# One order of query blocks for another: alternating block sizes, a longer look-ahead and later output units in an attention and mixture-of-experts kernel

## The chip, the cores and the metric

The kernel runs on one NeuronCore of one Trainium2 chip. The metric is the device time of one execution in microseconds. Every time below is from runs of the kernel before the change, or from one execution of it that the profiler recorded.

## What is computed

One layer: forgetting attention (softmax attention with a bias c[t]-c[s], the running sum of log-sigmoid forget gates), an output gate, a normalisation, a mixture of experts with top-2 routing, and a second normalisation. S = D = 1024, 16 heads of 64. The part that the change touches:

```python
proj = h @ w_in
q, k, v, f_logit, o_logit = jnp.split(...)
log_f = jax.nn.log_sigmoid((f_logit + b_f).astype(jnp.float32))
c = jnp.cumsum(log_f, axis=1)
...
logits = einsum('bqhd,bkhd->bhqk', q_i, k) * scale + c_i[..., :, None] - c[:, :, None, :]
logits = jnp.where(key_pos[None, :] <= q_pos[:, None], logits, -jnp.inf)
p = jax.nn.softmax(logits, axis=-1)
return einsum('bhqk,bkhd->bqhd', p, v)
...
o = merge_blocks(o) * jax.nn.sigmoid(o_logit)
return o @ w_out
```

## The kernel before

The values of all heads are computed first (`front`). Then `pairs` goes through eight pairs of heads (`hp` 0 to 7), and in each through eight query blocks of 128 rows (`i`) for each of the two heads (`j`): 16 steps a pair, 128 in all. A block `i` sees `i+1` blocks of 128 keys, so a block 7 has eight times the work of a block 0. Below, (hp: i,j) names a block, as (2: 0,0).

A block goes through two functions. `attn_s` (line 362) forms the logits with TensorE in a PSUM tile `sp` (two of these are there), takes their minimum on VectorE (`mn`; the sign of the logits is turned), takes the exponential on ScalarE (`s`), makes a high and a low fp16 part (`hl`: the copy of line 378 on ScalarE, the subtraction of line 379 on VectorE) and issues a DMA transpose of it from SyncE into `pT` (line 381). `attn_o` (line 385) multiplies `pT` with the values. Four blocks (two `i`, two `j`) share a PSUM tile `ops`; after the fourth, the group is finished: reciprocal `ro` and product `ox` on VectorE (lines 403 and 405), the gate on GpSimd (line 407), a copy `gh` on ScalarE (line 409), a subtraction `gl` on GpSimd (line 410). `ox` has one buffer. Two steps later, two DMA transposes (line 414, called "the turn" here) write the group into `oTh` and `oTl`, which the output projection reads.

The order is one list, `todo`. Blocks are started `LA` = 4 steps ahead of their `attn_o`, in `start`. Between the two, `fill` puts in TensorE units of 0.66 us each, by a running budget: in pairs 0 to 6 the projections of the next pair (`proj_units`: queries, keys, gates; two PSUM tiles `pj`), whose results `evac` (line 336) takes to SBUF with ScalarE and VectorE; in the last pair the first output units (`out_units`), half a row of tiles 0 to 3 each. An output unit with k = 7 needs `oTh` and `oTl` of the last pair, and carries its tile's number; `fill` takes it once `turned[7]` holds that number, that is once the turn has been issued. `later` holds work for a later step: the turns, the loads of weights two pairs ahead (`load_w`), and their splits (`load_split`).

```python
todo = [(hp, i, j) for hp in range(NP) for i in ((0,1,6,7,2,3,4,5) if hp < NP - 1 else range(NT)) for j in range(2)]
...
for n, (hp, i, j) in enumerate(todo):
    start(n + LA)
    ...
    due -= self.fill(due)
    self.now = n
    ...
    self.attn_o(hp, i, j, ready.pop(n), ps)
```

The framework keeps the order of each engine's own instructions fixed when the kernel is built; each engine works its list off in that order and waits at an instruction until what it needs is there. SyncE issues nearly all DMAs, the transposes among them, in one such list. `bias_rows` (line 288) fills four bias tiles once, before the first pair. `mid_begin` (line 477), before the last pair, loads and splits what follows attention. After attention come the rest of the output projection, the routing and the experts, whose weights are streamed in from HBM by DMAs that stand behind the last turn on SyncE.

Of the kernel before, what the change touches and what calls it, by code (L numbers as in the profile page):

```python
# [28 lines left out]
PS = 16384.0  # L29
VW = 2 * HD + 2  # L30
CW = (16.0, 2.0 ** -4, 2.0 ** -12)
BIG = 1e30
# [4 lines left out]
QG = 2  # L37
# [21 lines left out]
class Kern:  # L59
# [18 lines left out]
    def fill(self, us):  # L78
        done = 0
        while us > done and self.fill_q:  # L80

            at = next((n for n, u in enumerate(self.fill_q) if len(u) < 3 or u[2] in self.turned[NP - 1]), None)
            if at is None:
                break
            c, f = self.fill_q.pop(at)[:2]
            f()
            done += c
        return done
# [165 lines left out]
    def load_w(self, hp, step=None):  # L254
        nc = self.nc
        at = 0
        for n, off in self.QKG:
            h = self.wp.tile([128, KT, 128], F16, name="wh", bufs=3)
            l = self.wp.tile([128, KT, 128], F16, name="wl", bufs=3)
            self.W[hp, n] = (h, l)  # L260
            for c in range(2):
                def load(n=n, off=off, c=c):
                    r = self.wp.tile([128, 4, 128], F32, name="wr", bufs=3)
                    ks = slice(4 * c, 4 * c + 4)
                    nc.sync.dma_start(r, self.w_k[:, ks, off + hp * 128:off + (hp + 1) * 128])
                    return self.W[hp, n][0][:, ks, :], self.W[hp, n][1][:, ks, :], r
                if step is None:
                    self.split(*load(), WS, "pool")
                else:
                    self.load_split(load, step + (0, 2, 6, 8, 11, 13)[at])  # L270
                at += 1


    def load_split(self, load, step):
        def late(tiles):
            with self.tc.issue_after(self.mn.ins), self.tc.issue_after(self.gated.ins):
                self.split(*tiles, WS, "pool")
        self.later.append((step - 4, lambda: self.later.append((step, lambda t=load(): late(t)))))
# [9 lines left out]
    def bias_rows(self):  # L288
        nc, wk = self.nc, self.wk
        w = wk.tile([3, 2, S], F16, name="cw", tag="s", bufs=3)  # L290
        for n, sign in enumerate((1.0, -1.0)):
# [6 lines left out]
        for q, k in zip(self.QB, self.KX):  # L298
            for j in range(2):
                o = (1 - j) * 64  # L300
                nc.gpsimd.memset(q[o:o + 64, j, :], 0.0)
                nc.vector.memset(k[o:o + 64, 2 * j + 1, :], 0.0)
                nc.sync.dma_start(q[o:o + 3, j, :], w[:, 0, :])
                nc.sync.dma_start(k[o + 3:o + 6, 2 * j + 1, :], w[:, 1, :])
# [57 lines left out]
    def attn_s(self, hp, i, j, ps):  # L362
# [11 lines left out]
        self.mn = nc.vector.tensor_reduce(mn, sp[:, :n], axis=AX, op=OP.min)  # L374
        s = wk.tile([128, S], F32, name="s", bufs=3)
        nc.scalar.activation(s[:, :n], sp[:, :n], AF.Exp, scale=-1.0, bias=mn)  # L376
        hl = wk.tile([128, 2 * S], F16, name="hl", bufs=3)[:, :2 * n]
        nc.scalar.activation(hl[:, :n], s[:, :n], AF.Copy, scale=PS)  # L378
        nc.vector.scalar_tensor_tensor(hl[:, n:], s[:, :n], PS, hl[:, :n], op0=OP.mult, op1=OP.subtract)  # L379
        pT = wk.tile([128, 2 * NT, 128], F16, name="pT", bufs=5)[:, :2 * (i + 1), :]  # L380
        nc.sync.dma_start_transpose(pT, hl)
# [3 lines left out]
    def attn_o(self, hp, i, j, pT, ps):  # L385
# [3 lines left out]
        if i % nb == 0 and j == 0:  # L389
            self.o_ps = ps.tile([128, QG, 2, HD + 1], F32, name="ops", bufs=2)  # L390
        V = self.V[hd // 8]
        vo = hd % 8 * VW
        vh, vl = slice(vo, vo + HD + 1), slice(vo + HD + 2, vo + VW)
        o = self.o_ps[:, i % nb, j, :]
        for b in range(i + 1):
# [3 lines left out]
        if j == 0 or i % nb < nb - 1:  # L399
            return  # L400
        T = self.o_ps[:, :nb]
        r = wk.tile([128, QG, 2, 1], F32, name="ro", bufs=2)[:, :nb]
# [9 lines left out]
        def turn():  # L412
            for g, oT in ((gh, self.oTh), (gl, self.oTl)):
                nc.sync.dma_start_transpose(oT[:, hp, ts].rearrange("p (a b) -> p a b", b=128),
                                            g.rearrange("p a b c -> p (a b c)"))
            self.turned[hp].add(i)
        self.later.append((self.now + 2, turn))

    def pairs(self, ps):
        LA = 4  # L420
        self.bias_rows()
        self.later = []
        todo = [(hp, i, j) for hp in range(NP) for i in ((0,1,6,7,2,3,4,5) if hp < NP - 1 else range(NT)) for j in range(2)]
        per = len(todo) // NP
# [9 lines left out]
        def start(n):  # L434
            if n < len(todo):
                hp = todo[n][0]
                if n % per == 0:
                    while len(self.fill_q) > gates:
                        self.fill(0.1)
                    if hp + 1 < NP:  # L440
                        self.load_c(hp + 1)
                        if hp + 2 < NP:
                            self.load_w(hp + 2, n - LA + 11)
                        self.fill_q += self.proj_units(hp + 1)
# [27 lines left out]
        while self.later:  # L472
            self.later.pop(0)[1]()
        self.flush()

# [794 lines left out]
    def run(self):  # L1270
        tc, nc, I = self.tc, self.nc, self.I
        self.w_k = I["fox_w_in"].rearrange("a d c -> (a d) c").rearrange("(k p) c -> p k c", p=128)
        self.W, self.QA, self.SG = {}, {}, {}
        self.turned = [set() for _ in range(NP)]
        self.wo, self.OP = [None, None], {}
# [109 lines left out]
```

## Time and profile before

| | |
|---|---|
| runs shown | 1170.14, 1173.2 and 1164.64 us; median 1170.14 |
| the profiled execution | 1179.74 us, of which the span from first to last instruction is 1177.9 us |
| busy, TensorE / VectorE / ScalarE / GpSimd | 85% / 68% / 44% / 38% of the span |
| mean granted TensorE clock | 0.932 |
| attention | from 138 us (first logits) to 571 us (last product with the values) |

The table's busy shares are means over stages that differ. A matmul's busy time has a modelled end, so that matmuls in a row overlap: 512 columns are shown with 0.38 us, and the next one starts 0.216 us later. The time that TensorE has nothing to do is therefore read from what the profile lists as waits, or from start to start.

### The profile page before, as it was taken

The numbers are of one execution on the slowest core, as the hardware profiler recorded it, in microseconds if no ns is written. First come the engines' busy times: TensorE is split into PE (matmuls) and PEld (weight loads), VectorE is DVE, ScalarE is ACT, GpSimd is POOL, SyncE is SP. The second block draws the span as 40 slices with busy tenths as digits, with TensorE's granted clock in tenths as the row PEclk, the third lists the DMA queues.
The fourth block names the chain that finished last, engine by engine and source line by source line (L and its number), as shares of the span: only waits on it lengthen the run. The fifth ranks groups of instructions, "written<-read, shape, count | busy, mean of one in ns | idle before, by whom it ended". The sixth has DMA issues, their size and how long they took to land. (4 is left out here: it accounts for less than half of the span.)

```text
span 1177.9 us, 27374 instructions
## 1 busy us (share of the span) xinstructions
PE 995.7 (85%) x11246; PEld 703.0 (60%) x11246; DVE 798.1 (68%) x1408; ACT 523.9 (44%) x835; POOL 444.1 (38%) x438
## 2 busy tenths in 40 slices
PE   7799799999989998978789778889789888888860
PEld 3344466575765756554344666777677767776740
DVE  3423566767667786747499768767986767777765
ACT  4111456657666575735053544433343434443431
POOL 3400421222222322123110146666665666554453
PEclk9899899999999999989899979988989999989985
DMA  8900285778678687668776479999899999998560
GB/s 247 229 19 1 53 130 110 142 131 142 126 130 155 139 166 139 121 140 149 197 253 228 164 202 304 311 278 274 246 294 262 289 265 284 280 277 258 154 204 37
DMA packets 290467, 221.77 MB, mean 188 GB/s; under 512 B 207640, under 2 KB 232216, under 8 KB 290336
## 3 DMA queue, kind: packets, MB, share of 16 engines
q1 hardware_dynamic: 281120, 188.50, 62.3%
q0 software_dynamic: 8640, 29.37, 10.4%
q8 instruction: 90, 1.47, 0.5%
q10 hardware_dynamic: 576, 2.10, 0.4%
q14 instruction: 41, 0.34, 0.1%
HBM read 147.80 MB, written 23.69 MB: 146 GB/s over the span
## 5 line engine op out<-in xcount | busy, mean ns | idle before, releaser
L379 DVE SCALAR_TENSOR_TENSOR hl<-s,hl 128x256 f16<-128x256 f32 (+7 forms) x128 | 102.0, 797 | 83.6 <-ACT hl L378 81.9
L376 ACT ACTIVATE s<-sp,mn 128x256 f32<-128x256 f32 (+7 forms) x128 | 94.3, 737 | 90.0 <-DVE mn L374 88.1
L407 POOL TENSOR_TENSOR ox<-ox,sg 128x256 f32<-128x256 f32 (+1 forms) x36 | 32.0, 888 | 252.5 <-DVE ox L405 252.5
L374 DVE TENSOR_REDUCE mn<-sp 128x1 f32<-128x256 f32 (+7 forms) x128 | 95.2, 749 | 14.5 <-PE sp L372 13.4
L95 PE MATMUL pj<-xTh,wh 128*128 128x512 f16 x256 | 97.9, 382 | 7.1 <-ACT qa L351 7.1
L378 ACT ACTIVATE hl<-s 128x256 f16<-128x256 f32 (+7 forms) x128 | 87.3, 682 | 25.8 <-DMA pT<-hl 22.9
L97 PE MATMUL pj<-xTh,wl 128*128 128x512 f16 x256 | 97.8, 382 | 0.0
L96 PE MATMUL pj<-xTl,wh 128*128 128x512 f16 x256 | 97.8, 382 | 0.0
L95 PE MATMUL pj<-wh,xTh 128*128 128x128 f16 x512 | 92.5, 225 | 1.0 <-POOL wh L70 1.0
L96 PE MATMUL pj<-wl,xTh 128*128 128x128 f16 x512 | 92.5, 225 | 0.0
L97 PE MATMUL pj<-wh,xTl 128*128 128x128 f16 x512 | 92.5, 225 | 0.0
L940 POOL DMA_INDIRECT acc<-yr,dst x29 | 56.0, 1931 | 72.1 <-DMA raw<-in_moe_w_gate_dram 26.3
L95 PEld LDWEIGHTS <-xTh 128*128 128x128 f16 x704 | 69.5, 100 | 21.5 <-DMA xTh<-xhl 3.7
L96 PEld LDWEIGHTS <-xTh 128*128 128x128 f16 x704 | 69.3, 100 | 17.9 <-issue 3.2
L97 PEld LDWEIGHTS <-xTl 128*128 128x128 f16 x704 | 69.3, 100 | 16.9 <-issue 2.6
L396 PE MATMUL ops<-v,pT 128*128 128x65 f16 x576 | 66.9, 194 | 14.0 <-DMA pT<-hl 14.0
L860 ACT ACTIVATE hh<-t 128x160 f16<-128x160 f32 (+1 forms) x68 | 22.1, 327 | 127.1 <-DVE t L859 126.8
L369 PE MATMUL sp<-kx,qa 128*128 128x512 f16 (+2 forms) x192 | 62.4, 325 | 17.5 <-ACT s L376 17.1
L396 PEld LDWEIGHTS <-pT 128*128 128x128 f16 x576 | 54.5, 98 | 29.8 <-DMA pT<-hl 19.5
L397 PE MATMUL ops<-v,pT 128*128 128x64 f16 x576 | 67.0, 196 | 0.0
L398 PE MATMUL ops<-v,pT 128*128 128x65 f16 x576 | 66.6, 194 | 0.0
L821 POOL DMA_INDIRECT xg<-hl_d,idx x31 | 49.7, 1605 | 40.2 <-DVE gsum L706 18.0
(369 smaller groups left out, 3513.9 us busy)
## 6 DMA issues: line engine op xcount, KB each, us to landing
raw<-in_moe_w_up_dram SPq DMA_DIRECT2D x64, 512.0 KB
raw<-in_moe_w_down_dram SPq DMA_DIRECT2D x64, 512.0 KB
raw<-in_moe_w_gate_dram SPq DMA_DIRECT2D x60, 512.0 KB
wr<-in_fox_w_in_dram SPq DMA_DIRECT2D x48, 256.0 KB
xr<-in_x_dram SPq DMA_DIRECT2D x8, 512.0 KB
xh<-in_x_dram SPq DMA_DIRECT2D x16, 256.0 KB
wvr<-in_fox_w_in_dram SPq DMA_DIRECT2D x6, 512.0 KB
hl_d<-hlr SPq DMA_DIRECT2D x6, 512.0 KB
```

The lines of the kernel that those rows point to most:

```text
L95: nc.tensor.matmul(p, ah, bh, start=first, stop=False)
L96: nc.tensor.matmul(p, ah, bl, start=False, stop=False)
L97: return nc.tensor.matmul(p, al, bh, start=False, stop=last)
L369: nc.tensor.matmul(sp[:, ks], self.QA[hp][:, j, qb], self.KX[hp % 2][:, 2 * j, ks], start=True, stop=False)
L374: self.mn = nc.vector.tensor_reduce(mn, sp[:, :n], axis=AX, op=OP.min)
L376: nc.scalar.activation(s[:, :n], sp[:, :n], AF.Exp, scale=-1.0, bias=mn)
L378: nc.scalar.activation(hl[:, :n], s[:, :n], AF.Copy, scale=PS)
L379: nc.vector.scalar_tensor_tensor(hl[:, n:], s[:, :n], PS, hl[:, :n], op0=OP.mult, op1=OP.subtract)
L396: nc.tensor.matmul(o, pT[:, b, :], V[b][:, vh], start=(b == 0), stop=False)
L397: nc.tensor.matmul(o[:, :HD], pT[:, b, :], V[b][:, vl], start=False, stop=False)
L398: nc.tensor.matmul(o, pT[:, i + 1 + b, :], V[b][:, vh], start=False, stop=(b == i))
L940: self.nc.gpsimd.indirect_dma_start(out=self.acc, out_offset=bass.IndirectOffsetOnAxis(ap=self.dst[self.key(job, o)][:n, job[0]:job[0] + 1 ...
```

## The change

- The order within pairs 0 to 6 becomes `ORDER`: blocks 0 and 6 alternate, then 1 and 7, then 2 and 4, then 3 and 5. The last pair keeps 0 to 7.
- `LA` goes from 4 to 5, and `pT` has six buffers and not five. `s` has two and not three.
- Two groups are open at a time, so `o_ps` is kept by group; the two groups that run side by side are finished in steps that follow each other.
- An output unit that needs the last pair is held for three more steps: `turns[hp][i] = now + 3` when the turn is issued, and `fill` takes the unit when that step has come.
- The zeroing of the key side's bias tiles moves from VectorE to GpSimd. The splits of the weights take their steps as a list; `gated` may be unset at first.

```diff
--- before.py
+++ after.py
@@ -28,6 +28,7 @@
+ORDER = [(i, j) for p in ((0, 6), (2, 4)) for q in range(2) for j in range(2) for i in (p[0] + q, p[1] + q)]
@@ -79,7 +80,7 @@
-            at = next((n for n, u in enumerate(self.fill_q) if len(u) < 3 or u[2] in self.turned[NP - 1]), None)
+            at = next((n for n, u in enumerate(self.fill_q) if len(u) < 3 or self.turns[NP - 1].get(u[2], 1e9) <= self.now), None)
@@ -267,13 +268,13 @@
-                    self.load_split(load, step + (0, 2, 6, 8, 11, 13)[at])
+                    self.load_split(load, step[at])
...
-            with self.tc.issue_after(self.mn.ins), self.tc.issue_after(self.gated.ins):
+            with self.tc.issue_after(self.mn.ins), self.tc.issue_after(self.gated.ins) if self.gated else ExitStack():
@@ -287,7 +288,7 @@
-        w = wk.tile([3, 2, S], F16, name="cw", tag="s", bufs=3)
+        w = wk.tile([3, 2, S], F16, name="cw", tag="s", bufs=2)
@@ -299,7 +300,7 @@
-                nc.vector.memset(k[o:o + 64, 2 * j + 1, :], 0.0)
+                nc.gpsimd.memset(k[o:o + 64, 2 * j + 1, :], 0.0)
@@ -372,12 +373,12 @@
-        s = wk.tile([128, S], F32, name="s", bufs=3)
+        s = wk.tile([128, S], F32, name="s", bufs=2)
...
-        pT = wk.tile([128, 2 * NT, 128], F16, name="pT", bufs=5)[:, :2 * (i + 1), :]
+        pT = wk.tile([128, 2 * NT, 128], F16, name="pT", bufs=6)[:, :2 * (i + 1), :]
@@ -387,18 +388,18 @@
-            self.o_ps = ps.tile([128, QG, 2, HD + 1], F32, name="ops", bufs=2)
+            self.o_ps[i // nb] = ps.tile([128, QG, 2, HD + 1], F32, name="ops", bufs=2)
...
-        o = self.o_ps[:, i % nb, j, :]
+        o = self.o_ps[i // nb][:, i % nb, j, :]
...
-        T = self.o_ps[:, :nb]
+        T = self.o_ps[i // nb][:, :nb]
@@ -413,14 +414,17 @@
-            self.turned[hp].add(i)
+            self.turns[hp][i] = self.now + 3
         self.later.append((self.now + 2, turn))
 
     def pairs(self, ps):
-        LA = 4
+        LA = 5
+        self.gated = None
         self.bias_rows()
         self.later = []
-        todo = [(hp, i, j) for hp in range(NP) for i in ((0,1,6,7,2,3,4,5) if hp < NP - 1 else range(NT)) for j in range(2)]
+        self.o_ps = {}
+        todo = [(hp, i, j) for hp in range(NP) for i, j in
+                (ORDER if hp < NP - 1 else [(i, j) for i in range(NT) for j in range(2)])]
@@ -440,7 +444,7 @@
-                            self.load_w(hp + 2, n - LA + 11)
+                            self.load_w(hp + 2, [n - LA + 11 + m for m in (0, 2, 6, 8, 11, 13)])
@@ -471,6 +475,7 @@
         while self.later:
             self.later.pop(0)[1]()
+        self.now += 3
         self.flush()
```

The first place is VectorE where pair 1 passes into pair 2. The names there: `sp_2664` and `sp_2758` before are the logits of (1: 5,0) and (2: 0,0), `sp_2624` those of (1: 4,1); `kx0_977` takes the next pair's keys, `wl` a weight's low part. Before:

```order
L374 TENSOR_REDUCE mn_2630<-sp_2624 128x1
L355 SCALAR_TENSOR_TENSOR kx0_977<-pj_2498,kx0_977 64x512
L71 SCALAR_TENSOR_TENSOR wl_1910<-wr_2451,wh_1909 128x512
L355 SCALAR_TENSOR_TENSOR kx0_977<-pj_2498,kx0_977 64x512
L379 SCALAR_TENSOR_TENSOR hl_2634<-s_2632,hl_2634 128x640
L374 TENSOR_REDUCE mn_2670<-sp_2664 128x1
L374 TENSOR_REDUCE mn_2706<-sp_2700 128x1
L379 SCALAR_TENSOR_TENSOR hl_2674<-s_2672,hl_2674 128x768
L403 RECIPROCAL ro_2739<-ops_2614 128x4
L374 TENSOR_REDUCE mn_2762<-sp_2758 128x1
```

VectorE at the same place now, where `ops_2325` is the second of two groups that finish in neighbouring steps, `sp_2607`, `sp_2652` and `sp_2692` are the logits of (1: 5,0), (1: 3,1) and (1: 5,1), and `sp_2741` those of (2: 0,0):

```order
L404 RECIPROCAL ro_2598<-ops_2325 128x4
L406 TENSOR_TENSOR ox_2600<-ops_2325,ro_2598 128x256
L375 TENSOR_REDUCE mn_2613<-sp_2607 128x1
L72 SCALAR_TENSOR_TENSOR wl_1893<-wr_2453,wh_1892 128x512
L356 SCALAR_TENSOR_TENSOR kx0_977<-pj_2483,kx0_977 64x512
L375 TENSOR_REDUCE mn_2656<-sp_2652 128x1
L356 SCALAR_TENSOR_TENSOR kx0_977<-pj_2483,kx0_977 64x512
L380 SCALAR_TENSOR_TENSOR hl_2617<-s_2615,hl_2617 128x768
L380 SCALAR_TENSOR_TENSOR hl_2660<-s_2658,hl_2660 128x512
L375 TENSOR_REDUCE mn_2698<-sp_2692 128x1
L375 TENSOR_REDUCE mn_2745<-sp_2741 128x1
```

The logits of (2: 0,0) take the PSUM tile of the block two places ahead of it. Before, that block's minimum (`mn_2670`) stood behind both key subtractions and one of line 379; now the minimum of that block (`mn_2656`) stands between the two key subtractions.

The second place is TensorE in the last pair, at the first output unit that needs the last pair's own output (`pj_7370`, the last three matmuls of tile 0 with `oTh` and `oTl`); `sp_7420` are the logits of (7: 3,0). Before:

```order
L369 MATMUL sp_7420<-kx1_978,qa_6597 128x512
L370 LDWEIGHTS qb1_976
L370 MATMUL sp_7420<-kx1_978,qb1_976 128x512
L372 LDWEIGHTS identb_995
L372 MATMUL sp_7420<-mask_997,identb_995 128x128
L95 LDWEIGHTS oTh_66
L95 MATMUL pj_7370<-wo0_4805,oTh_66 128x512
L96 LDWEIGHTS oTh_66
L96 MATMUL pj_7370<-wo0_4805,oTh_66 128x512
L97 LDWEIGHTS oTl_67
L97 MATMUL pj_7370<-wo0_4805,oTl_67 128x512
```

TensorE where the same three matmuls (`pj_7381`) stand now; `sp_7574` are the logits of (7: 5,1), `pT_7408` is the block (7: 3,0):

```order
L371 MATMUL sp_7574<-kx1_978,qb1_976 128x256
L373 LDWEIGHTS identb_995
L373 MATMUL sp_7574<-mask_997,identb_995 128x128
L96 LDWEIGHTS oTh_66
L96 MATMUL pj_7381<-wo0_4828,oTh_66 128x512
L97 LDWEIGHTS oTh_66
L97 MATMUL pj_7381<-wo0_4828,oTh_66 128x512
L98 LDWEIGHTS oTl_67
L98 MATMUL pj_7381<-wo0_4828,oTl_67 128x512
L397 LDWEIGHTS pT_7408
L397 MATMUL ops_7600<-v10_74,pT_7408 128x65
```

They moved from beside the logits of (7: 3,0) to behind those of (7: 5,1), five blocks of logits later.

## Rows read from the trace of the kernel before

**Rows 1.** Windows, busy us by engine (instructions): pairs 0-6 summed, last pair, after it.

```profile
sum 358.62, PE 335.40 PEld 227.43 DVE 252.09 ACT 228.58 POOL 88.51; mean PE 47.91 PEld 32.49 DVE 36.01 ACT 32.65 POOL 12.64
...
496.79:571.30 74.51, 55.97 (x628) 35.25 (x628) 39.01 (x65) 31.82 (x50) 18.13 (x33) 0.88 0.76 148
...
600.00:650.00 50.00, 47.82 (x398) 23.87 (x397) 48.54 (x135) 20.18 (x21) 2.65 (x2) 1.00 0.66 233
```

**Rows 2.** Waits of TensorE, 138 to 509 us: who for whom, us, times, longest.

```profile
PE sp L369 <- ACT s L376: 16.3, 17, 2.1
PE ops L396 <- DMA pT<-hl: 4.7, 5, 1.5
```

**Rows 3.** Waits of TensorE, 509 to 576 us (last pair).

```profile
PE ops L396 <- DMA pT<-hl: 9.4, 5, 2.6
PE pj L95 <- DMA oTh<-gh: 7.3, 2, 5.9
PE pj L97 <- DMA oTl<-gl: 1.0, 2, 0.7
```

**Rows 4.** Timelines of VectorE, ScalarE and TensorE where pair 1 passes into pair 2.

```profile
233.17 0.69 DVE L355 SCALAR_TENSOR_TENSOR kx<-pj,kx 64x512 f16<-64x512 f32 x1
233.89 0.69 DVE L71 SCALAR_TENSOR_TENSOR wl<-wr,wh 128x512 f16<-128x512 f32 x1
235.05 0.69 DVE L355 SCALAR_TENSOR_TENSOR kx<-pj,kx 64x512 f16<-64x512 f32 x1 [0.47 <-ACT kx L354]
...
236.66 1.82 DVE L374 TENSOR_REDUCE mn<-sp 128x1 f32<-128x768 f32 x2
...
237.66 0.90 ACT L376 ACTIVATE s<-sp,mn 128x768 f32<-128x768 f32 x1 [1.88 <-DVE mn L374]
...
238.61 0.22 PE L369 MATMUL sp<-kx,qa 128*128 128x128 f16 x1 [2.07 <-ACT s L376]
```

**Rows 5.** Timeline of TensorE in the last pair, around the first output unit held up.

```profile
526.26 0.61 PE L95 MATMUL pj<-wo,oTh 128*128 128x512 f16 x1 [5.89 <-DMA oTh<-gh]
...
531.28 0.63 PE L95 MATMUL pj<-wo,oTh 128*128 128x512 f16 x1
531.70 0.63 PE L96 MATMUL pj<-wo,oTh 128*128 128x512 f16 x1
...
533.52 0.38 PE L95 MATMUL pj<-wo,oTh 128*128 128x512 f16 x1
533.73 0.38 PE L96 MATMUL pj<-wo,oTh 128*128 128x512 f16 x1
```

**Rows 6.** SyncE's transposes by tile, min/median/max ns: pT in pair 2; pT, oTh in the last.

```profile
L381 SPq DMA_TRANSPOSE pT<-hl x17: 1177/1347/2143, 240.4 to 291.5; - x17
...
L381 SPq DMA_TRANSPOSE pT<-hl x15: 1184/1559/3990, 506.8 to 565.7; - x15
...
L414 SPq DMA_TRANSPOSE oTh<-gh x9: 1095/1184/1690, 512.0 to 573.6; - x9
```

**Rows 7.** Timelines of VectorE and GpSimd: the finish of one group, first and last step.

```profile
200.90 0.42 DVE L405 TENSOR_TENSOR ox<-ops,ro 128x256 f32<-128x256 f32 x1
...
202.73 0.67 POOL L410 TENSOR_TENSOR gl<-ox,gh 128x256 f16<-128x256 f32 x1 [0.53 <-ACT gh L409]
```

**Rows 8.** Timelines of VectorE, TensorE and GpSimd at the entry into attention.

```profile
121.43 0.48 DVE L302 MEMSET kx<- 64x512 uint32 x1 [0.16 <-DVE wl L71]
...
127.02 0.56 DVE L306 CAST identb<-identf 128x128 bf16<-128x128 f32 x1
...
127.54 0.67 DVE L71 SCALAR_TENSOR_TENSOR wl<-wr,wh 128x512 f16<-128x512 f32 x1
...
142.22 0.69 DVE L355 SCALAR_TENSOR_TENSOR kx<-pj,kx 64x512 f16<-64x512 f32 x1
...
125.75 0.58 PE L95 MATMUL pj<-xTh,wh 128*128 128x512 f16 x1 [6.16 <-ACT qa L351]
...
126.55 3.96 POOL L301 MEMSET qb<- 64x1024 f16 x4
```

More of the change, by code (lines that the diff above doesn't have):

```diff
@@ L1273, in run @@
         self.W, self.QA, self.SG = {}, {}, {}
-        self.turned = [set() for _ in range(NP)]
+        self.turns = [{} for _ in range(NP)]
         self.wo, self.OP = [None, None], {}
```

## The prediction

> **What bounds the kernel now.** I read the windows by pair first. In pairs 0 to 6 TensorE is busy 335.4 of 358.6 us, so it has nothing to do for 23.2 us; VectorE is busy 36.0 us a pair, ScalarE 32.7, of 51.2 [rows 1]. A step is 358.6 / 112 = 3.2 us. The last pair is another stage: 74.5 us, TensorE busy for 56.0 of them, so 18.5 idle [rows 1]. TensorE sets the pace up to the last pair, and the change adds no matmul. What it can win is the idle time of TensorE, and the waits say whose it is: in pairs 0 to 6, 16.3 us in 17 waits of new logits for ScalarE to empty a tile `sp`, and 4.7 us in five waits for a transpose `pT` [rows 2]; in the last pair 9.4 us in five waits for `pT`, and 8.3 us (7.3 + 1.0) in four waits of an output unit for `oTh` or `oTl` [rows 3].
>
> After attention comes a stretch in which VectorE is busy 48.5 of 50 us [rows 1], and then the experts. What starts them (the first output tiles, and the weight loads behind the last turn on SyncE) hangs on the end of attention, so I let a gain there reach the end of the kernel in full.
>
> **The wait at the change of pairs.** Six times, once between every two pairs from pair 1 on, the logits of the new block (0,0) wait 2.1 us, the first at 238.61 [rows 4]. The row before them tells why: ScalarE's exponential of block (5,0) ended at 238.56, and it had waited for the minimum on VectorE, which stood behind a key subtraction, a weight split, a second key subtraction that itself waited for ScalarE, and a subtraction of line 379 (233.17 to 236.66). Now the tile that (0,0) takes is that of (3,1), whose minimum stands between the two key subtractions. Had the minimum stood there before, it would have begun when the weight split ended, at 233.89 + 0.69 = 234.58, and not at 236.66: 2.1 us earlier, all of the wait of 2.07. I take all six away: 6 x 2.07 = 12.4 us. At worst they come back in full (0). The other eleven waits of this kind hold 16.3 - 12.4 = 3.9 us; big blocks stood four in a row and now alternate with small ones, and I take 2 of it (0 to 3.9).
>
> **One step more of look-ahead.** A `pT` may now land 3.2 us later before TensorE misses it, and the longest of the five waits for it was 1.5 [rows 2]. All 4.7 us go (0 at worst). In the last pair the same five waits were up to 2.6 [rows 3], but there SyncE is close to full: of nine turns each has two transposes of 1.18 us, 21 us, and 15 `pT` of 1.56 at the median, 23 us and more, in some 65 us, with other loads between [rows 6]. The queue gets no shorter by looking further ahead, so I take half, 4.7 us (0 to 9.4).
>
> **Output units three steps later.** The first unit stood beside the logits of (7: 3,0), and TensorE waited 5.89 us in it [rows 5], with all that stood behind it, the logits of (7: 3,0) among them. It now stands five blocks of logits later, at least 5 x 3 = 15 us of TensorE's time. The 8.3 us go. Something comes with them: after the long wait the matmuls of 512 columns follow each other by 0.42 us (531.28 to 531.70), later by 0.21 (533.52 to 533.73) [rows 5]; that is the lower and the upper of the clock's two levels. Thirteen such matmuls ran at the lower one, 13 x 0.21 = 2.7 us, and I take them (0 to 2.7). What the held units cost: for two steps there is nothing to fill in between the products of block 3, and tile 2 must wait for tile 0's PSUM tile. This lies beside the queue of transposes, which sets the pace there, and I cost it at nothing; without that cover it would be a wait of some 2 us.
>
> **The entry.** Zeroing the key tiles leaves VectorE (0.48 us each [rows 8]) and joins GpSimd's list, where four fills of this size took 3.96 us, to 130.5 [rows 8]; four more end at 134.5, ahead of the first logits at 138.2. But the first query subtraction on VectorE now stands behind the two small mask instructions and the second weight split (127.02 to 128.21, 1.2 us) in place of one zeroing of 0.48 [rows 8], and TensorE waits for this chain (the 6.16 us): +0.7. The second block is now (0: 6,0), which needs the keys above 512. Their subtraction ended at 142.9 [rows 8], and TensorE, which has two blocks (0,0) of logits and few units ahead of it, would come there about 2 us after the first logits, at 140.2: a wait of up to 2.7 us, part of which other units fill. +2, between 0 and 4.
>
> **Two groups finish in neighbouring steps.** `ox` has one buffer, so the second group's product waits on VectorE until GpSimd has made `gl` of the first. From `ox` to the end of `gl` was 2.5 us (200.90 to 203.40) [rows 7], and the second group comes one step, 3.2 us, later: mostly covered. Behind it on VectorE stands the next minimum (`mn_2613`), and new logits wait for that. There are 14 such places; I take +2 in all. Nothing at the low end; at the high end 25 (first rival).
>
> The smaller parts: `s` with two buffers would hold an exponential only until the subtraction two blocks back is done, which stands ahead of that block's minimum anyway: nothing. Fewer idle gaps also mean that VectorE and SyncE have about 4 us a pair less, and waits that were hidden come up; I add 6, a little under 1 a pair.
>
> **The sum.** -12.4 - 2 - 4.7 - 4.7 - 8.3 - 2.7 + 0.7 + 2 + 2 + 6 = -24.1 us. The profiled execution took 1179.74 us (the span of 1177.9 and 1.84 around it), so 1155.6, or 2.0% less. It was 9.6 us slower than the median of the runs, 1170.14; 2.0% off that is 1146.
>
> **Rivals.**
> (a) The single buffer of `ox` decides, and the kernel gets slower. If the finish of the first group takes longer than a step, VectorE stands still, and the minimum behind it comes late, 14 times. For it: both steps on GpSimd can fall behind a VectorE subtraction of line 379, by estimate up to 1.25 us (a subtraction of 512 columns took 0.69 [rows 4], the widest has 1024); a chain of 5.0 us (2.5 + 2 x 1.25) makes VectorE stand 1.8 us, 14 x 1.8 = 25 us, and the six waits at the change of pairs would stay, since they are VectorE's lateness too. Against it: the measured 2.5 us, and the slack of a tile: it is wanted two steps, 6.4 us, after its logits, of which minimum and exponential take 1.8 (0.91 and 0.90 at 768 columns [rows 4]). Deciding point: a chain above 3.2 us. Time: only the held units win (-8.3 - 2.7), so 1170 - 11 + 2.7 + 25 = 1187.
> By the Trainium skill (SBUF — State Buffer, SBUF: two separate sides) a VectorE instruction with two SBUF inputs and a GpSimd instruction that reads SBUF exclude each other for their whole length. By that rule both of the chain's GpSimd steps can be held up so, and the case (a) would be the likely one. The trace bears it out in part only: 2.5 us for the whole finish in rows 7 leaves no room for such a wait there.
> (b) SyncE's transposes are the bound in all pairs. Sixteen `pT` of 1.35 and eight transposes of a turn at 1.19 are 31 of 51 us [rows 1, 6], and weights and bias rows come on top; two turns now come one behind the other, four transposes and 4.8 us in which no `pT` is issued. If this makes `pT` late, the waits for `sp` turn into waits for `pT`, and only the held units win: 1170 - 11 + 2.7 = 1162. Against it: one step more of look-ahead is 3.2 us, and big transposes no longer come in a row.
> (c) It goes better: no hidden waits come up, and all of the waits for `sp` and `pT` go: -16.3 - 4.7 - 9.4 - 8.3 - 2.7 + 0.7 = -41, so 1130.
> That the change doesn't take place as told is ruled out by the orders shown.
>
> **Chances.** My forecast 0.55, (c) 0.15, (b) 0.20, (a) 0.10. A measurement of this kernel can tell about 1% from no change, 11.7 us, so faster means under 1158.4. The forecast and (c) are faster; of (b) 0.17 is within 1% and 0.02 faster, of (a) 0.08 slower and 0.02 within. With 0.01 of (b) on the slow side: faster 0.72, the same 0.19, slower 0.09. The range reaches from just above (c) to past (b), 1131 to 1167, and leaves out (a) and the last of (c).
>
> **What would show it.** Right: the logits of the first block of each pair start without a wait in the trace; pairs 1 to 6 take about 48 us, not 51 to 52; no wait of an output unit for `oTh` before 560 us; the last pair under 65 us. Wrong: VectorE waiting at `ox` for GpSimd's `gl` by more than 1 us at a time (a); `pT` as the first name among TensorE's waits, with SyncE issuing without a break (b); a last pair of 74 us though its waits for `oTh` are gone; or an entry that is over 5 us later than 138.2.

## The result, and the profile after

The changed kernel took 1180.63 us at the median of 20 runs (1175.02 to 1187.47), the kernel before 1173.29 us beside it (20 runs, 1164.64 to 1179.13): ratio 1.0059, 95% interval 1.0038 to 1.0080. A second measurement (run e9 below) gave 1.0043 (1.0013 to 1.0074). That is half a per cent slower, where 24 us less were forecast. The profiled execution took 1179.19 us with a span of 1177.3, 1.4 us under the median of these runs; that of the kernel before, with 1179.74 us, is longer than each of its 20 runs. So the two profiles, 0.6 us apart, do not show the difference of the medians.

The windows of the changed kernel (pairs 0 to 6 summed, the last pair, after it), as in [rows 1]:

```profile
sum 359.92, PE 333.38 PEld 224.36 DVE 250.14 ACT 225.60 POOL 86.39; mean PE 47.63 PEld 32.05 DVE 35.73 ACT 32.23 POOL 12.34
...
496.30:571.10 74.80, 55.18 (x650) 36.29 (x647) 39.27 (x66) 31.43 (x50) 15.69 (x33) 0.89 0.79 149
600.00:650.00 50.00, 47.99 (x399) 24.05 (x398) 49.13 (x136) 20.16 (x21) 2.50 (x2) 1.00 0.66 228
```

Nothing was won where it was meant to be: 359.9 us for pairs 0 to 6 (358.6 before), 74.8 for the last (74.5 by [rows 1], whose window ends 0.7 us short of the last product; 75.2 to there). With 1.8 us less before the first logits and 0.3 more behind attention that makes the 0.6 us by which the two spans differ. TensorE's waits, 138 to 509 us and then 509 to 576, as in [rows 2, 3]:

```profile
PE sp L370 <- ACT s L377: 13.0, 19, 2.3
PE sp L370 <- DVE kx L356: 10.1, 6, 2.0
PE pj L96 <- DVE kx L356: 2.1, 1, 2.1
PE pj L96 <- ACT qa L352: 2.1, 3, 1.2
...
PE ops L397 <- DMA pT<-hl: 10.6, 4, 5.0
PE sp L370 <- ACT s L377: 5.8, 4, 2.4
PE pj L98 <- DMA oTl<-gl: 0.9, 1, 0.9
PE pj L96 <- DMA oTh<-gh: 0.2, 1, 0.2
```

The waits that were to go did go: `pT` is no longer in the first list, `oTh` and `oTl` fell from 8.3 to 1.1 us. Others stand in their place (the 2.1 us of `pj` for `kx` lie already in the last pair). One is new by name: keys (`kx`), 10.1 us. It is five waits of 1.9 to 2.0 us, one at the second block, (6,0), of pairs 2 to 6, and a short one at the entry. The timelines of TensorE, ScalarE and VectorE at one of them:

```profile
291.40 0.38 PE L371 MATMUL sp<-kx,qb 128*128 128x512 f16 x1
293.77 0.32 PE L370 MATMUL sp<-kx,qa 128*128 128x384 f16 x1 [1.99 <-DVE kx L356]
...
290.24 0.90 ACT L377 ACTIVATE s<-sp,mn 128x768 f32<-128x768 f32 x1 [1.75 <-DVE mn L375]
291.17 0.84 ACT L379 ACTIVATE hl<-s 128x768 f16<-128x768 f32 x1
291.92 1.00 ACT L355 ACTIVATE kx<-pj 64x1024 f16<-64x1024 f32 x1
...
293.03 0.68 DVE L356 SCALAR_TENSOR_TENSOR kx<-pj,kx 64x512 f16<-64x512 f32 x1
```

The half of (6,0) that needs keys up to 512 ran at 291.40; the other half stood until the last key unit, which TensorE had finished by 291, had passed ScalarE (behind an exponential and a copy) and VectorE.

The other 13.0 us wait for `sp`. Before, 12.4 of 16.3 us stood at the change of pairs, at (0,0); now 3.0 us stand there, 7.9 at the blocks (5,0) and (5,1), and the longest is one of these. Its chain, by the timelines of SyncE, ScalarE, VectorE and TensorE:

```profile
320.08 3.00 SPq L382 DMA_TRANSPOSE pT<-hl  x1
...
326.26 0.52 ACT L379 ACTIVATE hl<-s 128x384 f16<-128x384 f32 x1 [2.05 <-DMA pT<-hl]
...
327.41 0.59 ACT L350 ACTIVATE qa<-pj 64x512 f16<-64x512 f32 x1
...
329.62 0.79 ACT L377 ACTIVATE s<-sp,mn 128x640 f32<-128x640 f32 x1 [0.26 <-DVE mn L375]
...
326.82 0.56 DVE L380 SCALAR_TENSOR_TENSOR hl<-s,hl 128x384 f16<-128x384 f32 x1 [1.89 <-ACT hl L379]
328.04 0.69 DVE L351 SCALAR_TENSOR_TENSOR qb<-pj,qa 64x512 f16<-64x512 f32 x1 [0.66 <-ACT qa L350]
328.76 0.82 DVE L375 TENSOR_REDUCE mn<-sp 128x1 f32<-128x640 f32 x1
...
330.47 0.38 PE L370 MATMUL sp<-kx,qa 128*128 128x512 f16 x1 [2.30 <-ACT s L377]
```

Read it from the end. TensorE waits 2.30 us for an exponential; that waited for its minimum at 328.76; the minimum stood on VectorE behind a query subtraction (line 351), which waited 0.66 us for ScalarE's part of it, and behind the subtraction of line 380, which waited 1.89 us for ScalarE's copy into `hl`; on ScalarE both stood behind that copy; and the copy waited 2.05 us, because all three buffers of `hl` were still held. The transpose of the oldest had come to its turn on SyncE at 320.08 and left it at 323.08, and the copy began 3.2 us after that. ScalarE's waits for `hl` between 138 and 497 us, first the kernel before, then the changed one:

```profile
ACT hl L378 <- DMA pT<-hl: 18.4, 14, 3.0
```

```profile
ACT hl L379 <- DMA pT<-hl: 28.7, 22, 3.0
```

With copies and transposes matched one to one, `hl` is held from the start of its copy to the end of its transpose on SyncE for 4.27 us before and 5.15 after (means over the 96 blocks of pairs 1 to 6); of that the time between the subtraction's end and the transpose's start on SyncE is 1.14 and 1.89 us. The next copy into the same buffer began at the earliest 2.3 us (before) and 1.5 us (after) behind that end.

### The profile page after: what moved, and what is told of

Same layout as the page of the kernel before. It is cut to its first block, busy times and chain, and to the rows that moved or that the text cites. A ratio compares the mean times of both kernels' runs of the same rounds, so it can differ in the third digit from the quotient of the medians.

```text
span 1177.3 us, 27380 instructions
## 1 busy us (share of the span) xinstructions
PE 991.8 (84%) x11246; PEld 699.8 (59%) x11246; DVE 792.9 (67%) x1404; ACT 520.6 (44%) x835; POOL 440.8 (37%) x442
## 3 DMA queue, kind: packets, MB, share of 16 engines
q0 software_dynamic: 8640, 29.37, 10.3%
## 5 line engine op out<-in xcount | busy, mean ns | idle before, releaser
L380 DVE SCALAR_TENSOR_TENSOR hl<-s,hl 128x256 f16<-128x256 f32 (+7 forms) x128 | 99.6, 787 | 79.7 <-ACT hl L379 78.8
L96 PE MATMUL pj<-wh,xTh 128*128 128x128 f16 x512 | 89.1, 220 | 3.0 <-DVE kx L356 2.1
L97 PE MATMUL pj<-wl,xTh 128*128 128x128 f16 x512 | 89.1, 220 | 0.0
L98 PE MATMUL pj<-wh,xTl 128*128 128x128 f16 x512 | 89.1, 220 | 0.0
L370 PE MATMUL sp<-kx,qa 128*128 128x512 f16 (+3 forms) x192 | 63.0, 328 | 29.1 <-ACT s L377 18.9
L96 PEld LDWEIGHTS <-xTh 128*128 128x128 f16 x704 | 68.2, 98 | 23.1 <-DMA xTh<-xhl 3.1
L71 POOL TENSOR_SCALAR wh<-wr 128x512 f16<-128x512 f32 x48 | 34.3, 723 | 126.6 <-PE pj L97 61.2
L97 PEld LDWEIGHTS <-xTh 128*128 128x128 f16 x704 | 68.1, 98 | 16.2 <-issue 1.5
L408 POOL TENSOR_TENSOR ox<-ox,sg 128x256 f32<-128x256 f32 (+1 forms) x36 | 26.8, 744 | 135.4 <-DVE ox L406 135.4
L397 PE MATMUL ops<-v,pT 128*128 128x65 f16 x576 | 66.9, 194 | 10.6 <-DMA pT<-hl 10.6
```

Source lines behind the costliest of these rows:

```text
L96: nc.tensor.matmul(p, ah, bh, start=first, stop=False)
L97: nc.tensor.matmul(p, ah, bl, start=False, stop=False)
L98: return nc.tensor.matmul(p, al, bh, start=False, stop=last)
L370: nc.tensor.matmul(sp[:, ks], self.QA[hp][:, j, qb], self.KX[hp % 2][:, 2 * j, ks], start=True, stop=False)
L397: nc.tensor.matmul(o, pT[:, b, :], V[b][:, vh], start=(b == 0), stop=False)
```

## The experiments

What each left: ratio to the kernel before on the same chip with its interval; ScalarE's waits for `hl` from 138 to 497 us; the length of pairs 0 to 6 and of the last pair in the profile. LA is how far ahead logits run; `hl`, `pT` and `s` are numbers of buffers. The lengths are of one execution each: e1 and e7, which have the same code in pairs 0 to 6, differ there by 8.5 us, nearly all of it by the granted clock (last section). So the ratios decide, and a difference in length of that size shows nothing by itself.

| run | LA | hl | pT | s | ratio (95%) | hl waits us | pairs 0-6 | last |
|---|---|---|---|---|---|---|---|---|
| before | 4 | 3 | 5 | 3 | 1 | 18.4 | 358.6 | 75.2 |
| changed | 5 | 3 | 6 | 2 | 1.0059 (1.0038 to 1.0080) | 28.7 | 359.9 | 74.8 |
| e1 changed | 5 | 4 | 6 | 2 | 0.9881 (0.9839 to 0.9923) | 0.2 | 341.7 | 73.1 |
| e2 swap | 5 | 3 | 6 | 2 | 1.0063 (1.0033 to 1.0093) | 29.1 | 366.6 | 74.7 |
| e3 no hold | 5 | 3 | 6 | 2 | 1.0039 (1.0009 to 1.0068) | 35.3 | 365.5 | 72.6 |
| e4 | 4 | 3 | 5 | 3 | 1.0013 (0.9989 to 1.0038) | 10.8 | 361.2 | 74.1 |
| e5 before | 4 | 4 | 5 | 3 | 0.9928 (0.9899 to 0.9957) | 3.8 | 348.7 | 76.1 |
| e6 keys early | 5 | 4 | 6 | 2 | 0.9872 (0.9844 to 0.9901) | 13.3 | 345.1 | 71.4 |
| e7 no hold | 5 | 4 | 6 | 2 | 0.9891 (0.9860 to 0.9921) | 0.6 | 350.2 | 71.6 |
| e8 old order | 5 | 4 | 6 | 2 | 0.9906 (0.9872 to 0.9940) | 0 | 351.0 | 73.3 |
| e11 | 4 | 5 | 5 | 2 | 0.9985 (0.9962 to 1.0007) | 0 | 355.1 | 72.8 |
| e12 keys early | 4 | 5 | 5 | 2 | 0.9952 (0.9926 to 0.9977) | 0 | 349.0 | 74.6 |
| e13 s: 3 | 5 | 3 | 6 | 3 | 1.0016 (0.9995 to 1.0038) | 31.3 | 361.8 | 76.0 |
| e14 before | 4 | 2 | 5 | 3 | 1.0256 (1.0219 to 1.0293) | 58.0 | 386.3 | 78.1 |
| e15 keys early | 5 | 5 | 5 | 2 | 0.9831 (0.9801 to 0.9861) | 0.6 | 339.7 | 70.5 |

**e1: a fourth `hl`.**

```diff
-        hl = wk.tile([128, 2 * S], F16, name="hl", bufs=3)[:, :2 * n]
+        hl = wk.tile([128, 2 * S], F16, name="hl", bufs=4)[:, :2 * n]
```

> The changed kernel with a fourth buffer for hl (the split exponentials that SyncE transposes). Theory H: in pairs 0 to 6 the sp waits that are left (13.0 us, 19 times) come from ScalarE standing at its copy into hl until a transpose has read an older hl (28.7 us, 22 times, against 18.4 us, 14 times in the kernel before). Then ScalarE's waits for hl fall below 10 us, TensorE's sp waits below 7 us, attention ends 5 to 8 us earlier, and the time is 5 to 8 us under the changed kernel's 1180.6 us (ratio to the kernel before 0.999 to 1.001). Rival Q: VectorE's and ScalarE's queues are late whatever hl does (a minimum stands behind subtractions of the projections); then the waits at hl fall but TensorE's waits stay within 2 us, and so does the time. The waits for kx (10.1 us) stay by both.

Measured 0.9881, about 20 us under the changed kernel: theory H by the waits, with a gain that it put at 5 to 8 us. ScalarE's and TensorE's waits of this run (to 497 us):

```profile
ACT hl L379 <- DMA pT<-hl: 0.2, 1, 0.2
```

```profile
PE sp L370 <- DVE kx L356: 10.3, 6, 2.0
PE sp L370 <- ACT s L377: 3.2, 8, 0.6
```

From 13.0 to 3.2 us for `sp`; the `kx` waits stay. The last product of attention ends 20 us earlier, and from there to the end of the span it is 606.6 us, 605.9 in the kernel before: the gain reaches the end. The profiled execution is the fastest of six. Its pairs 0 to 6 are 18.2 us shorter: 12.4 us are TensorE's waits (26.2 and 13.8 us to 497 us), 5.7 its busy time (333.4 and 327.7); none of these pairs shows a granted clock under 1.00 here, and two show 0.97 in the changed kernel.

**e2: two blocks exchanged.**

```diff
+ORDER[1], ORDER[2] = ORDER[2], ORDER[1]
```

> The changed kernel with only the second and third block of each pair exchanged, so that a pair begins (0,0), (0,1), (6,0), (6,1). Theory K: the wait at the change of pairs did not go, it moved one block on: (6,0) needs the keys above 512 of the new pair, which the last projection unit before it leaves behind ScalarE's and VectorE's queue (kx, 10.1 us in 6 waits of up to 2.0 us, one in each of pairs 1 to 6). With (0,1) between, the kx waits fall below 3 us, attention ends 6 to 12 us earlier, and the time falls by as much (1169 to 1175 us by the changed kernel's 1180.6; ratio to the kernel before 0.996 to 1.001). Rival Q: the queues of VectorE and ScalarE are simply that late at this place, and the wait comes back as one for sp at (6,0) or (0,1): kx below 3 us, sp up by 8 us or more, time within 2 us of the changed kernel.

Measured 1.0063, as slow as the changed kernel. The waits to 497 us:

```profile
PE sp L371 <- ACT s L378: 19.1, 19, 2.4
PE pj L97 <- DVE kx L357: 8.9, 7, 3.1
PE sp L371 <- DVE kx L357: 0.4, 1, 0.4
```

The logits no longer wait for keys, but the next projection unit waits for the PSUM tile that the late subtraction still reads (`pj` for `kx`), and `sp` rose by 6 us, not 8. Rival Q: with three `hl` the place in the order decides nothing.

**e3 and e7: no hold**, with three and with four `hl`.

```diff
-            self.turns[hp][i] = self.now + 3
+            self.turns[hp][i] = self.now
```

> The changed kernel without the three blocks that the output units of the last pair wait after their transposes were issued. By the prediction this brings back some 8 us of waits at oTh and oTl in the last pair, and attention ends 5 to 8 us later. Rival E: the units are what covers the four last blocks; taken early they leave the end bare, taken late they fill it, and what the last pair takes is set by the chain of its own softmax and transposes: then the waits for oTh come back (5 us or more), the pT waits and sp waits (16.4 us now) fall by about as much, and the last pair stays within 3 us of 74.6.

> e1_hl4 without the three blocks that the output units wait. By the prediction 5 to 8 us slower than e1_hl4. By rival E, for which the run without the hold spoke (the last pair took 72.4 us instead of 74.6), within 3 us of e1_hl4, and waits for oTh of 4 us or more against fewer for pT.

e3 has the changed kernel's code up to the last pair, so its 365.5 us there are one more execution of that. Both last pairs are shorter without the hold (72.6 and 71.6 us, against 74.8 and 73.1; but with the hold 72.7 was seen too, in e16), and the times can't be told from those with it. In e3 `oTh` waits come back with 4.7 us and `pT` falls from 10.6 to 5.1. Rival E: the waits trade places.

**e4 and e11: four blocks ahead**, with three and with five `hl`.

```diff
-        LA = 5
+        LA = 4
-        pT = wk.tile([128, 2 * NT, 128], F16, name="pT", bufs=6)[:, :2 * (i + 1), :]
+        pT = wk.tile([128, 2 * NT, 128], F16, name="pT", bufs=5)[:, :2 * (i + 1), :]
```

(e4 also has three `s`; e11 has five `hl`.)

> The changed kernel with logits four blocks ahead, five buffers for pT and three for s, as in the kernel before; the alternating order and the held units stay. If the fifth block ahead is worth what the prediction gave it (part of the 9.4 us for pT waits), attention ends 3 to 6 us later than in the changed kernel. By theory H it is worth nothing, because hl is the shorter store: sp waits, pT waits and the time within 2 us of the changed kernel. If the second s buffer instead of the third costs something (ScalarE waited for VectorE at s 2.2 us, twice), it is up to 2 us faster.

> The changed kernel with five hl buffers instead of three, and for their room five pT, logits four blocks ahead. Theory H: hl is no limit any more at four (no wait for it in pairs 0 to 6 of e1_hl4), so the fifth gives nothing, and the fifth block ahead and the sixth pT are worth within 3 us: ratio to the kernel before 0.985 to 0.991 (e1_hl4: 0.988). If the fifth block ahead is worth the 4 us of the prediction, 0.991 to 0.995.

The two theories missed both times. With three `hl`, four ahead came out about 5 us faster than the changed kernel (the prediction had it slower, H the same, and only the clause on `s` the right way), but e4 has the third `s` too. The fair partner is e13 below, five ahead with three `s`: 1.0016, next to 1.0013 here. So with three `hl` the fifth block (and the sixth `pT` that e13 has) is worth nothing that shows, though ScalarE waits 31.3 us for `hl` with it and 10.8 without. With enough `hl`, four ahead (0.9985) is 12 us slower than e1: the fifth block is worth more than the prediction gave, but only when `hl` carries it. (e11 and e1 differ in `hl` and `pT` too; e12 and e15 below differ in LA alone.) In the profiles 9.7 of the 13.4 us between e11 and e1 in pairs 0 to 6 are busy time of TensorE: e11 shows a granted clock of 0.97 in four of these pairs and 0.94 in one, e1 1.00 in all.

**e5 and e14: the kernel before with four and with two `hl`.**

> The kernel before, with a fourth hl buffer and nothing else. Theory H: hl was the short store before the change too (ScalarE waited for it 18.4 us in 14 places of pairs 0 to 6). Then these waits fall below 5 us, the sp waits at the change of pairs (16.3 us, 17 times) fall by 6 us or more, and the time falls 8 to 15 us (ratio 0.987 to 0.993). Rival A: only the alternating order and the fifth block ahead make hl short (a block's hl is held 4.27 us from the copy to the end of its transpose before, 5.15 us after the change); then the kernel before gains 0 to 4 us (ratio 0.997 to 1.000).

> The kernel before with two hl buffers instead of three. Theory H: an hl is held 4.27 us from the start of its copy to the end of its transpose, and no next copy began under 2.3 us behind that end, so two buffers let a block through every 3.3 us at best, where a block now takes 3.25 us on the mean with strong swings; ScalarE's waits for hl rise from 18 us to 60 us or more, and the time by 20 to 60 us (ratio 1.017 to 1.05). If hl were not in the chain, the ratio stays under 1.005.

Two, three, four buffers: 1.0256, 1, 0.9928, and 58.0, 18.4, 3.8 us of ScalarE's waits (62.7 in e14 to 522 us, where its last pair begins), what theory H asked for but in one point: the `sp` waits fell by 5.2 us in e5, not 6. So `hl` was short before the change too. The waits at the change of pairs are for the most part another thing: 9.1 of their 12.4 us are left in e5, and three of the six stand as they were (TensorE in e5, at the start of pair 3):

```profile
284.20 0.22 PE L369 MATMUL sp<-kx,qa 128*128 128x128 f16 x1 [2.05 <-ACT s L376]
```

**e6, e12, e15: the keys one block earlier**, with LA and buffers by the table.

```diff
             if n < len(todo):
                 hp = todo[n][0]
+                if n % per == per - 1 and hp + 1 < NP:
+                    while len(self.fill_q) > gates:
+                        self.fill(0.1)
                 if n % per == 0:
```

> The changed kernel with four hl buffers, and the query and key units of the next pair emptied one block earlier than the change of pairs. Theory K: the kx waits (10.3 us, 6 times, of e1_hl4) come from the last key unit reaching ScalarE and VectorE too late; a block (some 3 us) earlier they fall below 3 us, attention ends 6 to 10 us earlier than in e1_hl4 and the time falls by as much (ratio to the kernel before 0.979 to 0.984). Rival Q, for which the exchange of two blocks spoke: the wait comes back for sp or for pj at the same place, and the time stays within 2 us of e1_hl4 (0.986 to 0.990).

> The same with the query and key units of the next pair emptied one block earlier, as in e6_hl4_kx. Theory: that run stood at the hl buffers again (13.0 us, 9 times) because all it had gained went into the store behind; with five these waits fall below 4 us, kx waits stay below 3 us, attention ends 4 to 8 us earlier than in e6_hl4_kx, ratio 0.979 to 0.984. Rival Q: the change of pairs costs VectorE and ScalarE the same work in any order; sp or pT waits take its place, and the ratio stays within 0.985 to 0.990.

> e6_hl4_kx (four hl, keys of the next pair one block earlier, logits five ahead) with five hl and, for the room, five pT. If hl alone is what that run stood at (13.0 us, 9 times), its waits go and the ratio falls to 0.979 to 0.985. If the sixth pT is what lets logits run five ahead, the waits move to SyncE (a transpose waits for the products to free its pT) and from there to pT at TensorE, and the ratio is 0.987 or more.

In e6 the `kx` waits went (0.2 us) and nothing was won (rival Q's time): `hl` was short again, by 13.3 us, and `sp` waits rose to 10.0. In e12 five `hl` took these waits, but four blocks ahead gave 0.9952 only, which neither side had. e15 differs from e12 in LA alone and gives 0.9831, as the first side said, the best of this study, 20 us under the kernel before. ScalarE's and TensorE's first waits of e6 (to 497 us):

```profile
ACT hl L379 <- DMA pT<-hl: 13.3, 10, 3.3
```

```profile
PE sp L370 <- ACT s L377: 10.0, 11, 1.6
...
PE sp L370 <- DVE kx L356: 0.2, 1, 0.2
```

ScalarE's and TensorE's waits of e15 (to 497 us):

```profile
ACT hl L379 <- DMA pT<-hl: 0.6, 1, 0.6
```

```profile
PE sp L370 <- ACT s L377: 5.7, 11, 0.9
PE ops L397 <- DMA pT<-hl: 3.4, 3, 2.2
PE sp L370 <- DVE kx L356: 0.3, 1, 0.3
```

With five `hl`, five `pT` are enough for five blocks ahead.

**e8: the old order**, with all else of e1.

> e1_hl4 with the blocks in the order of the kernel before (0, 1, 6, 7, 2, 3, 4, 5); five blocks ahead, six pT buffers, two for s and the held units stay. By the prediction the order alone brought 12.4 us, so this is 8 to 13 us slower than e1_hl4. By theories H and K the order only moved one wait at the change of pairs to another (10.3 us for kx now), so this is within 4 us of e1_hl4: kx waits below 3 us, sp waits at the change of pairs instead.

0.9906 against 0.9881: not told apart, so the 12.4 us that the prediction gave the order are not there. It has no `kx` waits and 19.5 us in 26 waits for `sp` of up to 1.1 us. In this pair of runs the order shows what it does to `hl` five blocks ahead: a block waits 1.13 us for SyncE in the old order and 2.74 in the new (means, as above). Four ahead it does not: 1.03 and 1.02 us in the new order (e4, e11), 1.14 in the kernel before. By these runs it takes the new order and the fifth block together; why is not tested.

**e13: the same room for a third `s`.**

> The changed kernel with the same 4 KB of room given to a third s buffer (as many as before the change) instead of a fourth hl. Theory H: it is hl that holds ScalarE's copies, so the third s gives less than 3 us of the 14 to 20 us that the fourth hl gave: ratio to the kernel before 1.001 to 1.007, waits for hl still 25 us or more in pairs 0 to 6. Rival B: the change is slower because it took the third s buffer, and any buffer in that chain gives the gain: ratio 0.987 to 0.995.

ScalarE still waits 31.3 us for `hl`, and the ratio is 1.0016, next to 0.9881 of e1: it is `hl`, not any buffer. Some 5 us of the loss may be the third `s` that the change took: e4 and e13, with three, are not told from the kernel before, and the runs with two `s` and three `hl` lie at 1.0039 to 1.0063. The intervals touch, so it is not shown.

**e9, e10, e16: second and third profiles** of the changed kernel and of the kernel before.

> The changed kernel again, unchanged, for a second profile. Its first profile ends attention 0.9 us before the kernel before, though by the medians it is 7 us slower. Theory V: the loss lies in pairs 0 to 6 and differs from one execution to the next with the transposes that hold hl (the run without the hold has the same code there and took 6 us longer); here the last pair then begins at 498 to 504 us instead of 496.3. Rival P: it lies behind attention, and from the last product to the end of the span it is 609 us or more, where the profiles of this study so far show 600.7 to 610.2. Ratio to the kernel before 1.003 to 1.009 by both.

> The kernel before again, for a second profile of it: ratio 0.998 to 1.002. Theory V: its pairs 0 to 6 vary less, the last pair begins at 494 to 498 us (496.8 in the first profile), the last product at 568 to 573 us.

> The changed kernel a third time, for one more profile of it. Theory V: the same program takes 360 to 366 us for pairs 0 to 6 (359.9, 361.8 and, without the hold, 365.5 us so far; 358.6 us twice in the kernel before), by how many pairs show a granted clock of 0.97 or 0.94, and the last pair 74 to 75 us.

Ratios 1.0043 for e9 and 0.9988 (0.9961 to 1.0015) for e10; e16 is a single execution. Pairs 0 to 6 took 359.9, 361.8 and 363.7 us in the changed kernel, 358.6 twice in the kernel before; the last pair takes 72.7 to 74.8 us for 75.2 and 76.8. Theory V had the lengths of pairs 0 to 6 right, and missed e10's last product (573.5 us) and e16's last pair (72.7). Rival P is out: 604.3 us from the last product in e9. Together the profiled executions differ by about 1 us in the span (means 1178.2 and 1177.1), not by the 5 to 7 us of the ratios. The choice of executions hides the rest: the two profiled ones of the kernel before took 6.5 and 2.4 us more than the medians of the runs beside them, the first two of the changed kernel 1.4 and 1.3 less. In which stage that loss lies stays open.

## Why the prediction was wrong

**The step that failed.** The sum took waits of TensorE away at the places where they showed and counted them as time won, without asking what stood ready behind them. Three parts of the sum are the miss, by the first profiles. The change of pairs, -12.4, came to +0.5. The other waits for `sp`, -2, came to +6.1 (3.9 us before, 10.0 now). The last pair, -4.7 - 8.3 - 2.7 = -15.7, came to -0.4.

**The store that the sum lacks.** The prediction's path went from `sp` to ScalarE's exponential and to VectorE's minimum. The copy into `hl` isn't on it, and neither is ScalarE's own wait there, 18.4 us in 14 places. At the change of pairs that it read, it was right as far as it went, for VectorE ran the subtraction of line 379 there without a wait.

```profile
235.81 0.82 DVE L379 SCALAR_TENSOR_TENSOR hl<-s,hl 128x640 f16<-128x640 f32 x1
```

But elsewhere the pairs are paced by this store: e5, e14 and e1 show it by taking and giving buffers. The change gave a buffer to `pT`, which e15 does without, and with the new order and the fifth block each block held its `hl` for longer. With a fourth `hl` (e1) 9.8 of the 13.0 us for `sp` went, and the kernel was 1.8% faster.

The Trainium skill (Perfetto Trace Analysis, Optimization Strategy) says that the same gap coming back over a stretch can mean that buffers for the next tile ran out. This case bears that out in part. With two, three and four `hl` in the kernel before TensorE waits 33.4, 16.3 and 11.1 us for `sp` (e14, before, e5), with the short buffer two engines away from it; but three of the six gaps of 2.1 us at the change of pairs stay with four.

**The change of pairs (-12.4).** The wait at (0,0) shrank, from 2.1 us to between 0.7 and 0.8 in four places and to nothing in two, as the order said; 9.8 us came back one block later, at (6,0), for `kx`. The prediction had priced keys above 512 at the entry (+2, measured 0.27 us) and put them at nothing for each new pair, which needs them in the same way. That they are a cause of their own is shown: a fourth `hl` leaves them (10.3 us in e1), and key units emptied a block earlier take them away (0.2 us in e6, 0.3 in e15).

**Look-ahead (-4.7 and -4.7).** In pairs 0 to 6 the `pT` waits went, as said, but TensorE now stood earlier in the same chain. Five ahead against four is worth 1.2% with five `hl` (e15, e12) and nothing with three (e13, e4, both with three `s`). In the last pair 10.6 us remain of 9.4: SyncE's queue was close to full there, as the prediction had said, and half was still too much. The timelines of VectorE, ScalarE, GpSimd, SyncE and TensorE in the changed kernel's last pair:

```profile
537.29 1.23 DVE L72 SCALAR_TENSOR_TENSOR wo<-wor,wo 128x1024 f16<-128x1024 f32 x1 [5.49 <-POOL wo L71]
...
556.21 1.36 DVE L380 SCALAR_TENSOR_TENSOR hl<-s,hl 128x1024 f16<-128x1024 f32 x1
...
524.52 1.06 ACT L69 ACTIVATE wo<-wor 128x1024 f16<-128x1024 f32 x1 [3.67 <-DMA wor<-in_fox_w_out_dram]
...
540.15 0.90 ACT L377 ACTIVATE s<-sp,mn 128x768 f32<-128x768 f32 x1 [7.48 <-DVE mn L375]
...
536.21 1.04 POOL L71 TENSOR_SCALAR wo<-wor 128x1024 f16<-128x1024 f32 x1 [4.12 <-DMA wor<-in_fox_w_out_dram]
...
564.54 3.24 SPq L382 DMA_TRANSPOSE pT<-hl  x1
...
526.40 0.38 PE L370 MATMUL sp<-kx,qa 128*128 128x512 f16 x1 [2.45 <-ACT s L377]
...
541.10 0.59 PE L370 MATMUL sp<-kx,qa 128*128 128x512 f16 x1 [2.01 <-ACT s L377]
...
569.60 0.23 PE L397 MATMUL ops<-v,pT 128*128 128x65 f16 x1 [4.99 <-DMA pT<-hl]
```

The last block's `hl` was ready at 556.21 + 1.36 = 557.6, its transpose was issued at 564.5, 7 us later, behind the rest of the transpose before it, a turn and a load, and TensorE waited 4.99 us for it.

**Output units (-8.3) and clock (-2.7).** The waits for `oTh` went as said, yet the last pair stayed at 74.8 us: the waits for `sp` rose from 0.9 to 5.8 us, and all of TensorE's waits there sum to 17.5 us instead of 18.6. Two of those for `sp` hang on output weights (`wor`) that `mid_begin` loads, and whose splits stand ahead of the softmax. At 541.10 it is a VectorE split that waited 5.49 us for GpSimd, which waited 4.12 us for the load, with minima behind it (ScalarE 7.48). At 526.40 it is ScalarE's part of another, which waited 3.67 us for its load, with an exponential behind it. No run takes these loads away, so this is read from the trace and not tested. A last pair of 74 us is the prediction's own sign of being wrong, and e3 and e7 show no gain from the hold. The granted clock of the last pair went from 0.88 to 0.89.

**Entry (+2.7) and `ox` (+2).** First logits at 136.38 instead of 138.17: nothing lost. Nor is the 1.8 us a gain that is shown: with the entry of the kernel before they come at 135.5 to 138.2 us (e10, e5, e14 too), with the changed one at 135.8 to 137.8 (e1, e3, e6, e9, e16 too). VectorE never waits at `ox` for `gl`; rival (a)'s reason is refuted, and that its time of 1187 lies nearer to the measured one than the forecast is luck. Rival (b) had the right queue and the wrong tile: SyncE's transposes are late, but what they keep is `hl`, and the wait shows at ScalarE, not as `pT` at TensorE. The 6 us for "waits that were hidden" were the place for all this, and far too small: in pairs 0 to 6, 1.9 us of the old waits for `sp` were to stay, with 2 for `ox` and these 6 beside them, 9.9 in all; 13.0 + 10.1 + 2.1 = 25.2 us for `sp`, `kx` and `qa` stand there.

**The end.** That a gain in attention reaches the end was right within some 10 us: behind the last product it is 600 to 611 us in all eighteen profiles of the study, while the last product itself comes between 548 and 600 us.

## What to carry to other kernels

A wait is read to its end: for the engine that is named, look up what it waited for itself, and go on until an engine is busy or a buffer is short. Look-ahead is worth what the shortest store in the chain lets through. Before adding a buffer to one tile, look for each tile of the chain at who waits for its buffers, and give the room to the one that is short (here one buffer for `hl` was worth 1.8%, the same room as `s` 0.4%, which is not told from nothing). The mean time that a tile is held does not show it: 5.15 us, and 2.5 us more until the next copy (the median of those that waited), are under the 9.6 us that three buffers at 3.2 us a block allow, and yet ScalarE waited 28.7 us for `hl`. A wait that an order removes has to be sought at the next instruction that needs the same late value.

## What the runs showed of the hardware that was not expected

The same code, with the same waits, is granted different clocks. Pairs 2 to 6 are one code in e1 and e7, and each has a wait of some 2 us for `kx`. Windows of pair 2 in e1, then in e7:

```profile
230.80:280.12 49.32, 47.03 (x568) 32.00 (x568) 35.62 (x55) 32.57 (x51) 13.02 (x17) 1.00 0.70 141
```

```profile
231.75:282.68 50.93, 48.66 (x568) 33.53 (x568) 35.61 (x55) 32.69 (x51) 12.97 (x17) 0.97 0.69 138
```

In e7 TensorE fell to the lower of its two levels (1.2 GHz) right behind that wait, as its timeline there shows by the steps of 128-column matmuls, 0.11 us at first and 0.06 later (in e1 they are 0.06 from the start):

```profile
238.22 0.31 PE L96 MATMUL pj<-wh,xTh 128*128 128x128 f16 x1
238.33 0.31 PE L97 MATMUL pj<-wl,xTh 128*128 128x128 f16 x1
...
241.27 0.22 PE L98 MATMUL pj<-wh,xTl 128*128 128x128 f16 x1
241.33 0.22 PE L96 MATMUL pj<-wh,xTh 128*128 128x128 f16 x1
```

It cost 1.6 to 1.9 us in each of five pairs of e7 and came in none of e1; in the kernel before three of the seven pairs of the first profile show 0.97 and two of the second. So a wait of 2 us cost 2 us in one execution and 3.6 or more in the other. Part of the spread between runs of one kernel may be this; no run tests it.
